# Weights' low part last in each granule, and a new order of products in the gates and the output projection

## The chip, the cores and the metric

The kernel runs on one core of a Trainium2 chip. Its engines are TensorE (PE, which multiplies matrices into the PSUM banks), VectorE (DVE), ScalarE (ACT), GpSimd (POOL) and SyncE (SP); SP and POOL issue the transfers from main memory (HBM). The metric is the device time of one execution in microseconds (us), lower is better.

## The reference

Two layers of a trunk on 512 tokens of 1024 channels, in float32:

```python
def swiglu(x, w_in, w_out):
    gu = x @ w_in
    g, u = jnp.split(gu, 2, axis=-1)
    return (jax.nn.silu(g) * u) @ w_out
...
    f = jnp.fft.fft2(ug, axes=(1, 3), norm="ortho").real
...
    y_na = neighbourhood_attention(q.reshape(shp), k.reshape(shp), v.reshape(shp), rpb) @ w_na_out
    y_f = fourier_mix(uf) @ w_f_out
    g_na = jax.nn.sigmoid(ga + gate_bias[0])
    g_f = jax.nn.sigmoid(gf + gate_bias[1])
    return (g_na * y_na + g_f * y_f) @ w_o
...
    for l in range(DEPTH):
        x = x + 0.5 * swiglu(rms_norm(x, ffn1_norm[l]), ffn1_w_in[l], ffn1_w_out[l])
        x = x + mixer(rms_norm(x, mix_norm[l]), mix_w_in[l], mix_gate_bias[l], na_rpb[l],
                      na_w_out[l], f_w_out[l], mix_w_o[l])
        x = x + 0.5 * swiglu(rms_norm(x, ffn2_norm[l]), ffn2_w_in[l], ffn2_w_out[l])
    return rms_norm(x, final_norm)
```

The hidden width of the feed-forward part (FFN) is 2816. `mix_w_in` makes q, k, v, the Fourier input u and two gates.

## The kernel before

*Two parts for each operand.* Every float32 operand a is split in a high part (a copy on ACT in the type fp32r) and a low part (a minus its high part, on DVE). A product is three matmuls into one sum: high by high, high activation by low weight, low activation by high weight (`mm3`, L333: L334, L335, L336 in this order). In the profile `whi` and `wlo` are the parts of weights, names that end in h and l those of activations.

*Strassen products.* Large products go by 2 x 2 blocks with seven products (1 to 7) for eight. The weights' operands of products 3, 5 and 6 are sums or differences, which are made on the way: on DVE (L182, a `Raw` tile and an `add`), or, where `strassen` (L219) is called with `dma`, by POOL transfers that add into the raw tile in place (`then`, L205; `Raw.plus`, L154).

*The stream of weights.* `stage_items` (L209) lists all granules (128 x 1024 raw numbers, 512 KB) in the order of use. `Stream` (L288) walks that list with four counters: `fetch` issues the loads on SP into a ring of raw tiles (9 in the FFN), `high` does the sum and the copy on ACT, `low` the subtraction on DVE (and the `then` transfer), and `next` hands out a granule after the two behind it have been made (`AHEAD`). `whi` and `wlo` have three buffers each. `negate` (L167) turns the sign of a raw tile on ACT and has POOL add another granule to it; this is done for the odd part of u (`un` minus `um`, tile uo) and for the cosine and sine sums of the Fourier output (`fq`).

*Granules and PE's order.* `product` (L479) takes two k-tiles of 128 in a granule for two PSUM banks, 12 matmuls of 512 columns (6 in a granule of one k-tile). `product_T` (L512) makes a transposed result for the gates, 24 matmuls of 256 columns a granule; with `fine` it is a generator that yields after each granule.

*The stages of a layer.* FFN (in-projection: `plain` in C tiles, then five column blocks in A, B; out-projection W_o, three chunks of k, tile o), mixer, FFN. The order of instructions is a scheduler's in the FFN. In the mixer (from the last part of W_o to the middle of the gates) the orders of DVE, ACT and PE are written by hand: what stands first in the code is first in the queue of its engine. There, in order: `proj_V` (v, whose parts are stored to HBM by SP, L982, and the folded inputs hp, hm, ex), `proj_U` (ue and ux, then uo), q, k and attention in steps `att_step` (L1270: output of head pair i-2, transposes of i-1, scores of i), with the Fourier output (`f_fill`, L1295, tile ef) between the last steps; then the gates: `block` and `block_1` are generators of the products of gate blocks 0 and 1, each `next` one granule or one product's end, with sums for the activations t1, t2, t3 and the rows of n (`fill_n`, tile ps) in between; last the output projection (L1590 to L1620: tiles wA, wB, wC, activations m1 to m7), and `put` adds into x.

The order of the gates' granules before is in one line of `stage_items`, which the sequence of `next(block)` and `next(block_1)` (L1545 to L1582) has to match:

```python
for i, order in ((0, (5,)), (1, (2,)), (0, (6, 7, 3)), (1, (5,)), (0, (4,)), (1, (6, 7, 3, 4))):
```

## Time and profile before

| | us |
|---|---|
| median of 3 runs (lowest to highest) | 1917.12 (1916.45 to 1921.8) |
| the profiled execution's own time | 1919.48 |
| its span in the trace | 1917.7 |
| PE busy, DVE busy, ACT busy | 1879.4, 1507.6, 1166.5 |

The first layer's stages lie so in the span: FFN's in-projection to 225 us, W_o to 338, v and u to 378, attention to 480, gates to 585, output to 610, the second FFN to 960. The second layer follows from 960 in the same order.

How to read it: busy times add up the instructions of an engine; matmuls are pipelined, so that one of 0.39 us is followed by the next after 0.23. A row of waits names the engine, the line and tile that waited, and after the arrow the engine and instruction that ended the wait; then the total, the number and the longest. A row of the timeline has start and duration in us, the engine, the line, the operation, out<-in and, in brackets, the idle time before it.

### The profile page before, as it was taken

The numbers are of one execution on the slowest core, as the hardware profiler recorded it, in microseconds if no ns is written. First come the engines' busy times: TensorE is split into PE (matmuls) and PEld (weight loads), VectorE is DVE, ScalarE is ACT, GpSimd is POOL, SyncE is SP. The second block draws the span as 40 slices with busy tenths as digits, with TensorE's granted clock in tenths as the row PEclk, the third lists the DMA queues.
The fourth block names the chain that finished last, engine by engine and source line by source line (L and its number), as shares of the span: only waits on it lengthen the run. The fifth ranks groups of instructions, "written<-read, shape, count | busy, mean of one in ns | idle before, by whom it ended". The sixth has DMA issues, their size and how long they took to land.

```text
span 1917.7 us, 25845 instructions
## 1 busy us (share of the span) xinstructions
PE 1879.4 (98%) x9609; PEld 1590.5 (83%) x9609; DVE 1507.6 (79%) x1902; ACT 1166.5 (61%) x1726; POOL 176.4 (9%) x212
## 2 busy tenths in 40 slices
PE   9999999999999999999999999999999999999997
PEld 7888888888997888888888888888888978888886
DVE  8767799757868777779977768995677797777898
ACT  6655666757565655566655556666675566555664
POOL 0101011000111000001000100110001110100010
PEclk9999999999999999999999999999999999999998
DMA  8777487855977476759857765977559875776693
GB/s 287 202 200 196 154 245 246 252 155 151 250 198 171 140 194 199 186 150 262 244 142 203 185 182 169 265 245 226 149 168 219 214 192 129 200 184 164 180 284 123
DMA packets 108301, 378.91 MB, mean 198 GB/s; under 512 B 12288, under 2 KB 12416, under 8 KB 108176
## 3 DMA queue, kind: packets, MB, share of 16 engines
q1 hardware_dynamic: 78944, 275.19, 41.2%
q0 software_dynamic: 28800, 101.78, 29.2%
q8 instruction: 75, 1.23, 0.3%
q14 instruction: 50, 0.41, 0.1%
q10 hardware_dynamic: 432, 0.30, 0.0%
HBM read 370.93 MB, written 6.29 MB: 197 GB/s over the span
## 4 chain that ended last, share of the span: by engine, by line
PE 73%; DVE 15%; issue 5%; ACT 4%; DMA 3%; POOL 0%; ACTq 0%; SPq 0%; DVEq 0%; POOLq 0%
PE A L334 7%; PE A L336 7%; PE A L335 7%; DVE wlo L197 5%; PE B L334 4%; PE B L336 4%; PE B L335 4%; PE o L335 3%; DMA raw<-in_wst_dram 3%; PE o L336 3%; PE o L334 3%; PE ps L334 2%; PE ps L336 2%; PE ps L335 2%; PE C L335 2%
## 5 line engine op out<-in xcount | busy, mean ns | idle before, releaser
L197 DVE TENSOR_TENSOR wlo<-raw,whi 128x1024 fp32r<-128x1024 f32 (+2 forms) x524 | 620.0, 1190 | 300.8 <-ACT whi L190 297.4
L190 ACT ACTIVATE whi<-raw 128x1024 fp32r<-128x1024 f32 (+2 forms) x524 | 539.2, 1033 | 441.9 <-PE A L336 116.6
L154 POOL DMA_DIRECT2D raw<-in_wst_dram x162 | 140.4, 875 | 1405.1 <-DMA raw<-in_wst_dram 768.2
L182 DVE TENSOR_TENSOR raw<-raw,raw 128x1024 f32<-128x1024 f32 (+1 forms) x128 | 150.9, 1189 | 2.5
L336 PE MATMUL A<-whi,xl 128*128 128x512 f32 x320 | 124.6, 389 | 0.0
L334 PE MATMUL A<-whi,xh 128*128 128x512 f32 x320 | 124.5, 389 | 0.0
L335 PE MATMUL A<-wlo,xh 128*128 128x512 f32 x320 | 124.5, 389 | 0.0
L188 ACT ACTIVATE whi<-raw 128x1024 fp32r<-128x1024 f32 x76 | 79.1, 1041 | 67.8 <-PE B L336 33.2
L195 DVE SCALAR_TENSOR_TENSOR wlo<-raw,whi 128x1024 fp32r<-128x1024 f32 x76 | 90.5, 1195 | 20.0 <-ACT whi L188 19.8
L543 ACT ACTIVATE sn<-A 128x512 f32<-128x512 f32 x96 | 56.5, 598 | 41.2 <-PE A L336 40.1
L336 PEld LDWEIGHTS A<-whi,xl 128*128 128x128 f32 x320 | 60.1, 188 | 12.5
L335 PEld LDWEIGHTS A<-wlo,xh 128*128 128x128 f32 x320 | 60.1, 188 | 12.5
L334 PEld LDWEIGHTS A<-whi,xh 128*128 128x128 f32 x320 | 60.1, 188 | 12.4
L334 PE MATMUL B<-whi,t1h 128*128 128x512 f32 x160 | 63.7, 398 | 0.0
L335 PE MATMUL C<-wlo,xh 128*128 128x512 f32 x160 | 62.4, 390 | 0.5 <-DVE wlo L197 0.5
L335 PE MATMUL A<-wlo,t2h 128*128 128x512 f32 x160 | 62.4, 390 | 0.4 <-DVE wlo L197 0.4
L334 PE MATMUL A<-whi,t3h 128*128 128x512 f32 x160 | 62.4, 390 | 0.2 <-ACT sn L543 0.2
L334 PE MATMUL C<-whi,xh 128*128 128x512 f32 x160 | 62.2, 390 | 0.2 <-ACT whi L190 0.2
L336 PE MATMUL B<-whi,t1l 128*128 128x512 f32 x160 | 62.4, 390 | 0.0
L335 PE MATMUL A<-wlo,t3h 128*128 128x512 f32 x160 | 62.3, 389 | 0.0
L336 PE MATMUL A<-whi,t2l 128*128 128x512 f32 x160 | 62.3, 389 | 0.0
L335 PE MATMUL B<-wlo,t1h 128*128 128x512 f32 x160 | 62.3, 389 | 0.0
(431 smaller groups left out, 5246.8 us busy)
## 6 DMA issues: line engine op xcount, KB each, us to landing
raw<-in_wst_dram SPq DMA_DIRECT2D x459, 512.0 KB
raw<-in_wst_dram POOLq DMA_DIRECT2D x180, 512.0 KB, 7.8
raw<-in_wst_dram SPq DMA_DIRECT2D x30, 256.0 KB
vc<-vd SPq DMA_DIRECT2D x28, 256.0 KB
bm<-in_near_dram SPq DMA_DIRECT2D x16, 384.0 KB
vd<-v SPq DMA_DIRECT2D x8, 512.0 KB
dft<-in_dft_dram POOLq DMA_DIRECT2D x4, 514.0 KB, 6.6
x<-in_xin_dram SPq DMA_DIRECT2D x4, 512.0 KB
```

The lines of the kernel that those rows point to most:

```text
L154: G.dma_start(out=self.t, in_=wst[GRAN_AT[self.plus]][:, 0 : self.n], accum_op=ALU.add)
L182: V.tensor_tensor(t, t, self.add.t, ALU.add)
L188: S.activation(self.out[0][:, cs], self.raw.t[:, cs], AF.Copy, scale=-1.0)
L190: S.activation(self.out[0][:, cs], self.raw.t[:, cs], AF.Copy)
L195: self.last = V.scalar_tensor_tensor(lo, t, -1.0, hi.bitcast(F32), ALU.mult, ALU.subtract)
L197: self.last = V.tensor_tensor(lo, t, hi.bitcast(F32), ALU.subtract)
L334: PE.matmul(ps, lh, rh, start=start, stop=False, skip_group_check=again)
L335: PE.matmul(ps, lh, rl, start=False, stop=False, skip_group_check=again)
L336: PE.matmul(ps, ll, rh, start=False, stop=stop, skip_group_check=again)
L543: S.activation(t[:, b, :], ps[b], AF.Copy)
```

## The change

`run` takes the place of `mm3` in `product`, `product_T`, `plain`, the last part of W_o, `proj_T`, `proj_V`, `proj_U`, `n_rows` and in half of `f_fill`. It takes a list of terms and first does, for each, high by high and the activation's low part by the weights' high part, and then, for each, the weights' low part:

```diff
+    def run(terms, again=False):
+
+        for ps, lh, ll, rh, rl, w, start, stop in terms:
+            PE.matmul(ps, lh, rh, start=start, stop=False, skip_group_check=again)
+            PE.matmul(ps, *((lh, rl) if w == "l" else (ll, rh)), start=False, stop=False, skip_group_check=again)
+        for ps, lh, ll, rh, rl, w, start, stop in terms:
+            PE.matmul(ps, *((ll, rh) if w == "l" else (lh, rl)), start=False, stop=stop, skip_group_check=again)
```

In `product` the terms of a granule go together, but those of the last granule go bank by bank, so that the first bank ends at its half (`product_T` alike):

```diff
+            if i + n == len(kts):
+                run(terms[0:n], again)
+                run(terms[n:], again)
+            else:
+                run(terms, again)
```

The sum of an item becomes a method of its own, which `low` calls for the next item, if that is loaded, ahead of its own subtraction:

```diff
         def low(self):
+            if self.prepped + 1 == self.highs < self.loaded:
+                self.items[self.highs].sum()
             self.items[self.prepped].low()
```

The gates' products and the output's:

```diff
-            for i, order in ((0, (5,)), (1, (2,)), (0, (6, 7, 3)), (1, (5,)), (0, (4,)), (1, (6, 7, 3, 4))):
+            for i, order in ((0, (5,)), (1, (2,)), (0, (6, 7)), (1, (5,)), (0, (3, 4)), (1, (6, 7, 4, 3))):
...
-            strassen(s, lambda q: "w" + q, 0, two, ORDER, True)
+            strassen(s, lambda q: "w" + q, 0, two, ORDER_W, True)
```

`ORDER_W` is (5, 1, 2, 6, 7, 3, 4), where `ORDER` was (1, 5, 2, 6, 7, 3, 4). For it, the sum of product 3 is not made by a POOL transfer into the tile of product 6 but by a DVE sum with b. In the code of the output, a2 and wB (product 5) now stand ahead of a6 and wA (product 1).

In `proj_V`, at two places of the attention, and in the first FFN, loads, negations and preparations move:

```diff
+            ws.fetch(ws.highs + 5)
             root = norm.roots(0, 2)
...
             h0 = upper(folds[0], "hp")
+            ws.negate()
+            ws.negate()
             done(2, False)
...
             ws.high()
-            ws.negate()
             some((0, 1), VG[2], False, False)
...
             ws.high()
-            ws.negate()
...
         att_step(2)
+        ws.fetch(ws.highs + 5)
+        ws.negate()
         r64, w64 = rows_64()
...
         bias_for(3)
+        ws.fetch(ws.highs + 5)
         ws.negate()
         att_step(4, lambda: ws.prep(ws.pos + 2))
-        ws.negate()
         ws.prep(ws.pos + 3)
...
-        att_step(5, ws.low, mid=lambda: next(f_rows))
-        for _ in range(3):
+        att_step(5, ws.low)
+        for _ in range(4):
             next(f_rows)
         ws.high()
-        att_step(6, ws.low, mid=lambda: next(f_rows))
-        ws.prep(ws.pos + 1)
-        for _ in range(3):
+        next(f_rows)
+        att_step(6, ws.low)
+        for _ in range(5):
             next(f_rows)
         ws.high()
-        att_step(7, ws.low, ws.high, ws.low)
+        att_step(7, ws.low, ws.prep_one)
...
-        fill_n(0, [ws.next(0), ws.next(0)])
+        fill_n(0, [ws.next(0), ws.next(0)], ws.prep_one)
         acts[6] = low(h2, t12, "t2")
-        ws.high()
-        ws.low()
```

`prep_one` is `high` and then `low`; `fill_n` calls it before its third row. `f_fill` yields before it drains a block instead of after it. In the first FFN `ws.prep(ws.pos + 3)` stands one DVE and ACT group earlier. The number of instructions of PE, and of loads on SP, stays.

More of the change, by code (lines that the diff above doesn't have):

```diff
@@ L33 @@
 ORDER_0 = (1, 2, 5, 6, 7, 3, 4)
+ORDER_W = (5, 1, 2, 6, 7, 3, 4)
 FETCH = (8, 4)
@@ L179, in high, with sum @@
                 )
-            t = self.raw.t
-            if self.add:
-                V.tensor_tensor(t, t, self.add.t, ALU.add)
+            self.sum()
             if self.parts == 1:
                 self.upper(slice(0, n))
+        def sum(self):
+            if self.add:
+                V.tensor_tensor(self.raw.t, self.raw.t, self.add.t, ALU.add)
+                self.add = None
         def upper(self, cs):
@@ L217, in strassen @@
         def strassen(s, name, idx, sizes, order, dma=False):
-            r = made.setdefault((s, name("a"), idx), {}) if dma and order[0] > 2 else {}
+            r = made.setdefault((s, name("a"), idx), {}) if dma and len(order) < 7 and order[0] > 2 else {}
             for q, q2 in () if r else (("a", None), ("b", None), ("c", "a"), ("d", "c")):
@@ L231, in strassen @@
                     elif m == 3:
-                        add(d, None if dma else b)
+                        add(d, None if dma and order is not ORDER_W else b)
                     elif m == 4:
@@ L237, in strassen @@
                     elif m == 6:
-                        add(d, None if dma else a, then=b.key if dma else None)
+                        add(d, None if dma else a, then=b.key if dma and order is not ORDER_W else None)
                     else:
@@ L315, in prep, with prep_one @@
                 self.low()
+        def prep_one(self):
+            self.high()
+            self.low()
         def enter(self, stage):
@@ L486, in product @@
             for b in range(2):
+                terms = []
                 for i, kt in enumerate(kts):
@@ L490, in product @@
                     last = stop and i == len(kts) - 1
-                    mm3(ps[b], h[:, kt, c], l[:, kt, c], wh[:, z], wl[:, z], start and i == 0, last, again)
+                    terms.append((ps[b], h[:, kt, c], l[:, kt, c], wh[:, z], wl[:, z], "r", start and i == 0, last))
+                run(terms, again)
                 if hook and b == 0:
@@ L499, in product @@
             wl = wl.rearrange("p (a b) -> p a b", b=T)
+            terms = []
             for b in range(2):
@@ L503, in product @@
                     lh, ll = h[:, kts[i + k], c], l[:, kts[i + k], c]
-                    mm3(
-                        ps[b], lh, ll, wh[:, k, :], wl[:, k, :], start and i + k == 0,
-                        stop and i + k == len(kts) - 1, again,
-                    )
+                    terms.append((
+                        ps[b], lh, ll, wh[:, k, :], wl[:, k, :], "r", start and i + k == 0,
+                        stop and i + k == len(kts) - 1,
+                    ))
+            if i + n == len(kts):
+                run(terms[0:n], again)
+                run(terms[n:], again)
+            else:
+                run(terms, again)
             if hook and i == 0:
@@ L516, in product_T @@
             wh, wl = [z.rearrange("p (a b c) -> p a b c", a=2, c=P) for z in (ws.next(0) if fine else ws.next())]
+            terms = []
             for cb in range(4):
@@ L521, in product_T @@
                     mh, ml = h[:, kt, off : off + 256], l[:, kt, off : off + 256]
-                    first = start and kt == 0
-                    PE.matmul(to, wh[:, k, cb], mh, start=first and cb % 2 == 0, stop=False, skip_group_check=True)
-                    PE.matmul(to, wh[:, k, cb], ml, start=False, stop=False, skip_group_check=True)
-                    PE.matmul(to, wl[:, k, cb], mh, start=False, stop=kt == 3, skip_group_check=True)
+                    first = start and kt == 0 and cb % 2 == 0
+                    terms.append((to, wh[:, k, cb], wl[:, k, cb], mh, ml, "l", first, kt == 3))
+            for n in (slice(0, 4), slice(4, 8)) if g else (slice(0, 8),):
+                run(terms[n], True)
             if fine:
@@ L581, in plain @@
             i, k = divmod(kt, 4)
+            terms = []
             for j in js:
@@ L584, in plain @@
                     t = slice((2 * j + b) * P, (2 * j + b + 1) * P)
-                    mm3(pcl[j][b], hx[i][:, k, t], lx[i][:, k, t], wh[:, c], wl[:, c], kt == 0, kt == DT - 1)
+                    terms.append((pcl[j][b], hx[i][:, k, t], lx[i][:, k, t], wh[:, c], wl[:, c], "r", kt == 0, kt == DT - 1))
+            run(terms)
         for g in range(2):
@@ L613, in stage_ffn @@
                 norm.squares(1, 0)
+            if first:
+                ws.prep(ws.pos + 3)
             V.tensor_tensor(b21, b21, b22, ALU.subtract)
@@ L618, in stage_ffn @@
                 norm.squares(1, 1)
-                ws.prep(ws.pos + 3)
                 norm.rstd()
@@ L755, in granule @@
                 kts = list(range(len(CHUNK[0][c])))[2 * g : 2 * g + 2]
+                terms = []
                 for b in bs:
@@ L758, in granule @@
                         t, z = slice(off + b * P, off + (b + 1) * P), slice(k * T, (k + 1) * T)
-                        mm3(
-                            to[b], h[:, kt, t], l[:, kt, t], w[0][:, z], w[1][:, z], False,
-                            c == 2 and g == 1 and k == len(kts) - 1, True,
-                        )
+                        terms.append((
+                            to[b], h[:, kt, t], l[:, kt, t], w[0][:, z], w[1][:, z], "r", False,
+                            c == 2 and g == 1 and k == len(kts) - 1,
+                        ))
+                run(terms, True)
             m, c, src = steps[i + 2]
@@ L952, in proj_T @@
             wh, wl = ws.next()
+            terms = []
             for kt in range(DT):
                 c = slice(kt * P, (kt + 1) * P)
-                mm3(ps, wh[:, c], wl[:, c], *xs[kt], kt == 0, kt == DT - 1)
+                terms.append((ps, wh[:, c], wl[:, c], *xs[kt], "l", kt == 0, kt == DT - 1))
+            run(terms)
             return ps
@@ L966, in some @@
             def some(cs, g, first, last):
+                terms = []
                 for k, (wh, wl) in enumerate(wide(w[g])):
@@ L970, in some @@
                         lh, ll = [z[:, c * P : (c + 1) * P] for z in xs[kt]]
-                        mm3(pss[c], lh, ll, wh, wl, first and k == 0, last and k == 1)
+                        terms.append((pss[c], lh, ll, wh, wl, "r", first and k == 0, last and k == 1))
+                run(terms)
             vt = {}
@@ L1070, in proj_U @@
                 wh, wl = [z.rearrange("p (a b) -> p a b", b=UC) for z in ws.next(0)]
+                terms = []
                 for n, kt in enumerate(kts):
@@ L1074, in proj_U @@
                         c = slice(b * P, (b + 1) * P)
-                        mm3(
-                            ps[b][:, 0:UC], hp[i][0][:, k, c], hp[i][1][:, k, c], wh[:, n, :], wl[:, n, :],
+                        terms.append((
+                            ps[b][:, 0:UC], hp[i][0][:, k, c], hp[i][1][:, k, c], wh[:, n, :], wl[:, n, :], "r",
                             kt == 0, kt == DT - 1,
-                        )
+                        ))
                     PE.matmul(px[0:2, 0:UC], ex[i][:, k, :], wh[:, n, :], start=kt == 0, stop=False)
+                run(terms)
+                for n, kt in enumerate(kts):
+                    i, k = divmod(kt, 4)
                     PE.matmul(px[0:2, 0:UC], ex[i][:, k, :], wl[:, n, :], start=False, stop=kt == DT - 1)
@@ L1096, in proj_U @@
                 wh, wl = [z.rearrange("p (a b) -> p a b", b=HALF) for z in ws.next(0)]
+                terms = []
                 for b in range(2):
@@ L1099, in proj_U @@
                     for k in range(4):
-                        mm3(
-                            ps[b][:, 0:HALF], hm[g][0][:, k, c], hm[g][1][:, k, c], wh[:, k, :], wl[:, k, :],
+                        terms.append((
+                            ps[b][:, 0:HALF], hm[g][0][:, k, c], hm[g][1][:, k, c], wh[:, k, :], wl[:, k, :], "r",
                             g == 0 and k == 0, g == 1 and k == 3,
-                        )
+                        ))
+                run(terms)
             for b in range(2):
@@ L1190, in bias_for, with att_scores @@
                 bms[hp].append(res)
-        def att_scores(i, after, mid):
+        def att_scores(i, after):
             hp, pr = divmod(i, 2)
@@ L1223, in att_scores @@
                     V.reciprocal(rs[:, 2 * e : 2 * e + 2], sm[:, 2 * e : 2 * e + 2])
-                    if mid and not e:
-                        mid()
             se = s_[0].rearrange("p (a k) -> p a k", a=2)
@@ L1268, in stage_mixer, with att_step @@
         sc, pt_ = {}, {}
-        def att_step(i, then=None, before=None, last=None, mid=None):
+        def att_step(i, then=None, before=None, last=None):
             if 0 <= i - 2 < 8:
@@ L1279, in att_step @@
             if i < 8:
-                sc[i] = att_scores(i, last, mid)
+                sc[i] = att_scores(i, last)
         fs, ns = {}, {}
@@ L1311, in f_fill @@
                         PE.matmul(pe, eh[:, c], pl, start=False, stop=False, skip_group_check=True)
-                        PE.matmul(pe, el[:, c], ph, start=False, stop=False, skip_group_check=True)
                     c = slice(i * T + cb * P, i * T + cb * P + P)
                     PE.matmul(pe, w64[0:68, c], p64[0][0:68, 0:KC], start=False, stop=False, skip_group_check=True)
+                    cs = [slice(gp * T + cb * P, gp * T + cb * P + P) for gp in range(2)]
                     for gp in range(2):
-                        c = slice(gp * T + cb * P, gp * T + cb * P + P)
-                        mm3(po, oh[:, c], ol[:, c], qf[gp][:, 0, :], qf[gp][:, 1, :], False, gp == 1, True)
+                        PE.matmul(pe, el[:, cs[gp]], pf[gp][:, 0, :], start=False, stop=False, skip_group_check=True)
+                    run([(po, oh[:, cs[gp]], ol[:, cs[gp]], qf[gp][:, 0, :], qf[gp][:, 1, :], "l", False, gp == 1) for gp in range(2)], True)
+                    yield
                     t = tmp(s="fo")[:, 0:HALF]
@@ L1323, in f_fill @@
                     V.tensor_tensor(y[:, T - 1 : HALF : -1], pe[:, 1:HALF], t[:, 1:HALF], ALU.add)
-                    yield
+                    if cb == 3:
+                        yield
         def n_rows(w, cb):
             ps = bank()
+            terms = []
             for kt, (h_, l_) in enumerate(o):
@@ L1331, in n_rows, with fill_n @@
                 c = slice(kt % 2 * T + cb * P, kt % 2 * T + cb * P + P)
-                mm3(ps, wh[:, c], wl[:, c], h_, l_, kt == 0, kt == 3)
+                terms.append((ps, wh[:, c], wl[:, c], h_, l_, "l", kt == 0, kt == 3))
+            run(terms)
             return ps
-        def fill_n(i, w):
+        def fill_n(i, w, then):
             for cb in range(4):
+                if cb == 2:
+                    then()
                 if cb % 2 == 0:
@@ L1470, in stage_mixer @@
         ga0, gf0, ga1, gf1 = [None, None], [None, None], [None, None], [None, None]
-        block = gate_block(0, acts, ORDER_0, {6: lambda: fourth()}, ga0, gf0, (1, 2, 5, 6))
-        block_1 = gate_block(1, acts, ORDER_0, {}, ga1, gf1, (1, 2))
+        block = gate_block(0, acts, (1, 2, 5, 6, 7, 3, 4), {6: lambda: fourth()}, ga0, gf0, (1, 2, 5, 6))
+        block_1 = gate_block(1, acts, (1, 2, 5, 6, 7, 4, 3), {}, ga1, gf1, (1, 2))
         ws.high()
-        att_step(5, ws.low, mid=lambda: next(f_rows))
-        for _ in range(3):
+        att_step(5, ws.low)
+        for _ in range(4):
             next(f_rows)
         ws.high()
-        att_step(6, ws.low, mid=lambda: next(f_rows))
-        ws.prep(ws.pos + 1)
-        for _ in range(3):
+        next(f_rows)
+        att_step(6, ws.low)
+        for _ in range(5):
             next(f_rows)
         ws.high()
-        att_step(7, ws.low, ws.high, ws.low)
+        att_step(7, ws.low, ws.prep_one)
         next(block)
@@ L1538, in stage_mixer @@
         ws.high()
+        ws.low()
         V.tensor_tensor(t12, t12, B[1, 1][1], ALU.add)
         next(block_1)
-        ws.low()
         h2 = high(t12, "t2")
-        fill_n(0, [ws.next(0), ws.next(0)])
+        fill_n(0, [ws.next(0), ws.next(0)], ws.prep_one)
         acts[6] = low(h2, t12, "t2")
-        ws.high()
-        ws.low()
         ws.high()
@@ L1577, in stage_mixer @@
         written.pop().__exit__(None, None, None)
-        for _ in range(2):
-            next(block)
+        next(block)
         next(block_1)
+        next(block)
         next(block)
@@ L1589, in stage_mixer @@
         m10, m11 = ga1
-        pa = pair("wA")
-        product(pa, a1, K4, True)
-        put(pa, 0, 0, -1)
-        a6 = combo(m00, m00, m11, ALU.add, "m6")
         a2 = parts(m10, "m2")
@@ L1597, in stage_mixer @@
         put(pb, 1, 1, -1)
+        a6 = combo(m00, m00, m11, ALU.add, "m6")
+        pa = pair("wA")
+        product(pa, a1, K4, True)
+        put(pa, 0, 0, -1)
         V.tensor_tensor(m01, m01, m11, ALU.subtract)
```

## The prediction

> **What bounds the kernel now.** I read first the page's busy times, then the list of what TensorE waited for, then the timeline at the largest of those waits, and last a table of windows by stage.

> ```profile
> span 1917.7 us, 25845 instructions
> PE 1879.4 (98%) x9609; PEld 1590.5 (83%) x9609; DVE 1507.6 (79%) x1902; ACT 1166.5 (61%) x1726; POOL 176.4 (9%) x212
> ```

> TensorE is busy for 98% of the span. The change leaves its 9609 matmuls and 9609 weight loads, so it can win only idle time, and time in which the clock is not full. By the page that is 1917.7 − 1879.4 = 38.3 us idle. Where it lies (columns: total us, times, longest):

> ```profile
> PE o L335 <- DVE wlo L197: 3.7, 7, 0.6
> PE ef L336 <- DVE wlo L197: 3.5, 2, 1.7
> PE B L523 <- ACT whi L190: 3.2, 2, 1.9
> ...
> PE ps L1239 <- DVE s L1227: 2.6, 4, 1.1
> PE uo L335 <- DVE wlo L197: 1.8, 2, 0.9
> PE uo L334 <- ACT whi L190: 1.7, 2, 1.1
> PE B L525 <- DVE wlo L197: 1.5, 2, 0.8
> PE ps L336 <- DVE wlo L197: 0.8, 2, 0.4
> PE wC L334 <- ACT m2h L340: 0.7, 2, 0.3
> PE wB L334 <- ACT whi L190: 0.7, 2, 0.3
> PE ux L1079 <- ACT ex L1048: 0.5, 1, 0.5
> PE C L335 <- DVE wlo L197: 0.5, 1, 0.5
> PE A L335 <- DVE wlo L197: 0.4, 1, 0.4
> ...
> PE C L334 <- ACT whi L190: 0.2, 1, 0.2
> ```

> Most are waits for a weights' low part (wlo), which DVE makes last of all operands of a granule. What one costs shows at the first W_o product with activation c6 (start, duration, instruction, idle before):

> ```profile
> 283.13 0.39 PE L334 MATMUL o<-whi,c6h 128*128 128x512 f32 x1
> ...
> 284.10 0.50 PE L335 MATMUL o<-wlo,c6h 128*128 128x512 f32 x1 [0.59 <-DVE wlo L197]
> ...
> 284.44 0.40 PE L336 MATMUL o<-whi,c6l 128*128 128x512 f32 x1
> 284.67 0.39 PE L334 MATMUL o<-whi,c6h 128*128 128x512 f32 x1
> ```

> Undisturbed matmuls of this shape start 0.23 us apart (284.44 to 284.67). Here one starts 284.10 − 283.13 = 0.97 us after the one before, and the next 0.34 after that. So the wait costs 0.74 + 0.11 = 0.85, the list's 0.59 and 0.26 more. I add 0.26 to every wait listed.

> Beside idle time there are stretches at half clock (columns after the window: us; busy of PE, PEld, DVE, ACT, POOL; granted clock; DMA share; GB/s):

> ```profile
> 460.00:520.00 60.00, 58.22 (x442) 55.48 (x443) 49.23 (x76) 38.78 (x77) 10.44 (x12) 1.00 0.85 225
> 531.00:539.00 8.00, 6.86 (x32) 6.66 (x33) 7.43 (x10) 5.35 (x10) 1.73 (x2) 0.57 0.48 109
> 1323.00:1328.00 5.00, 4.63 (x26) 4.63 (x27) 3.45 (x6) 2.81 (x5) 0.00 (x0) 0.66 1.00 388
> 1484.00:1488.00 4.00, 3.91 (x20) 3.91 (x21) 4.00 (x7) 2.65 (x5) 0.86 (x1) 0.57 0.46 137
> ```

> The first row, with ef's wait of 1.7 us in it, is at full clock. [...]

> **The change part by part.** *Low parts last.* In each granule all products with the high part go first, those with wlo last. In a granule of 12 matmuls the first use of wlo moves from place 2 to place 9, 7 × 0.23 = 1.6 us later; in the last granule of a product, which goes by halves of 6, from 2 to 5, 0.7. The price is that an activation's low part is wanted 0.23 earlier and that wlo's last use is one matmul later, hence its buffer. Matmuls keep their spacing whatever operand stands still: each has its own weight load already, so the new order costs PE nothing by itself.

> W_o has seven waits, 3.7 + 7 × 0.26 = 5.5 us, none over 0.6 listed, 0.85 in full, against 0.7 to 1.6 of new allowance: I take 5.0. The first FFN's three (C, A on wlo, and a 0.2 on whi that its earlier preparation should cover) are 1.1 + 0.8 = 1.9. W_o is also where the sum of the next granule, now done before the current low part, stands at another place in DVE's order; it is the same instruction, so no term of its own. Its cover is thin, since DVE is nearly full there:

> ```profile
> 225.00:338.00 113.00, 111.79 (x509) 92.33 (x508) 109.41 (x126) 73.46 (x94) 13.06 (x16) 1.00 0.80 240
> 560.00:608.00 48.00, 47.28 (x262) 40.49 (x260) 42.12 (x50) 27.38 (x37) 6.38 (x8) 1.00 0.80 192
> L197 DVE TENSOR_TENSOR wlo<-raw,whi 128x1024 fp32r<-128x1024 f32 (+1 forms) x37 | 41.6, 1136 | 2.4 <-ACT whi L190 2.4
> ```

> (The last row is DVE's group of low parts in the first of these windows.)

> *uo, earlier fetch and negation.* The raw weights of uo are loaded by SP behind the store of v, and summed by a POOL transfer after a negation on ACT:

> ```profile
> SPq L982 <- DVE v L981: 21.9, 2, 21.8
> 362.23 0.88 POOL L169 DMA_DIRECT2D raw<-in_wst_dram  x1 [21.31 <-ACT raw L168]
> 370.37 1.06 ACT L190 ACTIVATE whi<-raw 128x1024 fp32r<-128x1024 f32 x1 [1.90 <-DMA raw<-in_wst_dram]
> ```

> The transfer issued at 362.23 landed at 370.37, 8.1 us. Both loads now stand ahead of that store, which held SP for up to 21.8 us, and the negations ahead of at least four ACT instructions of 1.0 us (the copies of two products, h1's high part, a weights' high part), so the sum that landed at 370.4 should land near 366, and ACT waited for it 1.9. What is passed on SP, the v store here and loads of bm at the attention's fetches, comes one 512 KB load later, 2.3 us at the 225 GB/s of the row for 460 to 520; bm is wanted steps later, so I charge nothing, and 2.3 a layer if that cover is gone. All waits on uo and the one on ux go: 1.8 + 1.7 + 0.5 + 5 × 0.26 = 5.3, and the half-clock stretch at 1323 with them, 1.4. Together 6.7; I take 6.4.

> *Gates' third product.* Its two waits in each layer are B on whi and on wlo, 3.2 + 1.5 + 4 × 0.26 = 5.7, with stretches at 531 and 1484 worth 2.8 + 1.4 = 4.2:

> ```profile
> 529.04 0.28 PE L524 MATMUL B<-xl,whi 128*128 128x256 f32 x1
> 529.16 0.28 PE L525 MATMUL B<-xh,wlo 128*128 128x256 f32 x1
> 531.38 0.39 PE L523 MATMUL B<-xh,whi 128*128 128x256 f32 x1 [1.94 <-ACT whi L190]
> ...
> 532.64 0.58 PE L525 MATMUL B<-xh,wlo 128*128 128x256 f32 x1 [0.76 <-DVE wlo L197]
> ACT whi L190 <- DMA raw<-in_wst_dram: 5.4, 1, 5.4
> raw<-in_wst_dram POOLq DMA_DIRECT2D x4, 512.0 KB, 9.3
> ```

> The high part waited 5.4 us for one of four POOL transfers (last row, median 9.3 to land). Behind block 1's fifth product, 48 matmuls that start 0.12 apart (529.04 to 529.16), the third is wanted 5.8 us later, more than 1.94 + 0.76. The transfers of block 1's own sums, and one for the output product's first, now queue on POOL before others of block 1, 9.3 us each in turn, but block 1's third product, which needs the last, is now the last of all; its seventh runs straight into the fourth on one accumulator, and must wait for the subtraction on DVE (0 hidden, up to 1.22, the longest DVE row below); for that I charge 0.6 a layer. Term: 5.7 + 4.2 − 1.2 = 8.7.

> *Attention's filling.* ef and s are 3.5 + 2.6 + 6 × 0.26 = 7.7 over two layers. The weights' chain was:

> ```profile
> 459.02 1.08 ACT L340 ACTIVATE p<-ps 128x512 fp32r<-128x512 f32 x2
> 459.92 1.22 DVE L197 TENSOR_TENSOR wlo<-raw,whi 128x1024 fp32r<-128x1024 f32 x1
> ```

> The negations leave the ACT work ahead of it, about one instruction of 1.0 each, but the low part still stands behind the attention output on DVE. Bounds: nothing, or 3.8 a layer; I take 1.4 a layer, 2.8, near the lower since ef's wait is the larger and stays mostly.

> *Rows of n.* DVE had, up to the wait on the last:

> ```profile
> 491.14 1.22 DVE L1500 TENSOR_TENSOR t1l<-t,t1h 128x1024 fp32r<-128x1024 f32 x1
> 492.36 1.23 DVE L197 TENSOR_TENSOR wlo<-raw,whi 128x1024 fp32r<-128x1024 f32 x1
> ```

> The new order puts one such instruction of 1.22 more before two of the low parts, while low-last gives 0.5 to 1.4. Bounds: 0.8 a layer won (0.4 + 0.26, and what hangs on it), or 1.7 lost; I take 0.9 lost, 1.8 in all.

> *Output product.* wC and wB, 0.7 + 0.7 + 4 × 0.26 = 2.4, should go, as m2's parts are now made ahead of two products and m6's sum ahead of one, and a product is 24 matmuls of 0.23, 5.5 us. Four POOL sums become DVE adds, two a layer. At 1.22 (the first row of the last fence) they are 4.9 us on DVE, which has 48 − 42.1 = 5.9 idle in the stretch of a layer: hidden, 0; unhidden 4.9. I take them as hidden, and the term as 2.4. The raw tiles of these adds also hold their buffers longer, so some later load starts later; that is in the allowance below.

> Sum: 5.0 + 1.9 + 6.4 + 8.7 + 2.8 − 1.8 + 2.4 = 25.4. Against it stand waits that a list of today's can't name, above all on DVE's new order: none, or, by the dearest that I charge above (0.9 a layer in n) at two more places in each layer, 3.6; I take 2.4, nearer that end. Net 23 us. The profiled execution took 1919.5 (span 1917.7 and 1.8 around it), 2.4 over the median of 1917.1. It would take 1896.5; from the median, the forecast is **1894**.

> The half-clock rows stand each right after waits of 1.94 + 0.76, 0.5 + 1.1 + 0.9 and 1.3 + 0.8. [...]

> **The rivals.**
> (1) *Half clock stays*, for instance set off by other waits (ef, 1.7, at a place where n or the gates add to it). For: two of the three stretches came after waits of at most 1.3 each, and ef's is 1.7. Against: ef's own set off none. Time 1894 + 5.6 = 1900.
> (2) *DVE becomes the bound* in W_o and the output product. For: 109.4 of 113 us. Then W_o's 5.0 and the output's 2.4 are not won and the four adds cost 4.9: 1894 + 12.3 = 1906. Against: in the W_o window DVE's own idle is behind ACT's whi, not PE.
> (3) *The transfers slide along*: uo and the third product wait for data (POOL, 9.3 us, in turn), and earlier issue only lengthens their queue. Then 6.4 + 8.7 are lost: 1909. Against: at 524 to 531 only four transfers were under way.
> (4) *Slower: low parts block DVE.* Three wlo buffers; each is now free one matmul (0.23) later, and everything behind a waiting low part on DVE waits too. The W_o window has 37 low parts and there are four such stages: 148 × 0.23 = 34 us, time 1928. It turns the sign once the mean is over 23 / 148 = 0.16 us. Against: today DVE is the late one there, 2.4 us idle in 37, so it hardly finds a buffer still in use.

> **How the numbers follow.** Chances: forecast 0.63, (1) 0.08, (2) 0.13, (3) 0.09, (4) 0.07. A difference of 0.3%, 5.8 us, is about what can be told from none, so *same* is 1911.4 to 1922.9. Faster: 0.63 + 0.08 + 0.11 of (2) + 0.05 of (3) = 0.87; same the rest of these, 0.06, and a little of (4): 0.07; slower 0.06. The low end takes no new waits and n at its better bound: 23 + 2.4 + 3.4 of n + 3 of ef = 32, 1885. The high end reaches over (2) to (3), 1910.

> **What would show it.** In the changed kernel's list of waits: o on wlo (3.7) under 0.8; uo and ux gone; B on whi and wlo gone, and the granted clock at full through 520 to 560; ef still some 1.8 a layer; ps of the n rows larger, about 1 a layer; wC and wB gone. PE's instructions stay at 9609. Wrong would be: a new wait of PE on wlo in W_o (2), B or uo still waiting behind a transfer (3), DVE idle before wlo with PE as releaser (4), half clock away from these places (1).

## The result and the profile after

| | before | changed |
|---|---|---|
| median, us (4 runs each) | 1917.02 | 1905.56 |
| lowest to highest, us | 1916.45 to 1921.8 | 1903.99 to 1907.35 |
| profiled execution, us (its span) | 1919.48 (1917.7) | 1903.99 (1902.2) |

The ratio is 0.9935 (95% interval 0.9916 to 0.9954): faster, by 11.5 us between the medians where 23 was forecast, and inside the stated range. The two profiled executions lie 15.5 apart; before's was above its median and the changed kernel's was its fastest.

From the page of the changed kernel:

```profile
span 1902.2 us, 25942 instructions
PE 1874.4 (99%) x9609; PEld 1587.8 (83%) x9609; DVE 1513.3 (80%) x1906; ACT 1163.3 (61%) x1726; POOL 172.9 (9%) x208
```

PE's instructions are the same; DVE has four more and POOL four fewer. The changed kernel's list of what PE waited for (total us, times, longest; lines have moved, L351, L352 and L354 are high by high, low activation and low weight):

```profile
PE wB L351 <- ACT whi L194: 3.7, 2, 1.9
...
PE ef L354 <- DVE wlo L201: 2.9, 2, 1.5
PE ps L354 <- DVE wlo L201: 1.4, 2, 0.9
PE C L354 <- DVE wlo L201: 1.2, 2, 0.6
PE ps L1280 <- DVE s L1268: 0.9, 4, 0.3
PE A L351 <- ACT sn L570: 0.6, 2, 0.4
PE o L354 <- DVE wlo L201: 0.4, 1, 0.4
PE ps L351 <- ACT whi L194: 0.2, 1, 0.2
```

Without the warm-up's 3.2, the list went from 22.5 to 11.3 us. Gone are uo, ux, B, wC and all but one wait of o. At the top is now wB, 1.9 in each layer, which had 0.7 in both before and which the prediction had gone. The windows of the changed kernel where half clock was or is (columns as in the prediction, the granted clock third from the end):

```profile
520.00:560.00 40.00, 39.56 (x324) 38.85 (x323) 29.71 (x33) 23.99 (x37) 6.18 (x7) 1.00 0.87 229
602.00:605.00 3.00, 3.00 (x8) 2.34 (x7) 3.00 (x4) 1.06 (x1) 0.00 (x0) 0.50 0.87 294
1323.00:1328.00 5.00, 5.00 (x34) 3.89 (x34) 2.35 (x8) 2.09 (x5) 0.00 (x0) 1.00 0.52 182
1484.00:1488.00 4.00, 4.00 (x36) 4.00 (x35) 1.97 (x3) 2.50 (x4) 0.87 (x2) 1.00 0.37 142
```

The three old stretches are at full clock; one new one stands behind the wait of wB in the first layer.

To lay the terms of the prediction beside the trace, I took from both traces how much later each matmul starts than its shape's undisturbed spacing (0.227 us for 512 columns, 0.120 for 256, 0.109 for transposes), counted what is over 0.095, kept matmuls in half clock apart, and added by stage, over both layers:

| stage | lost before + half clock | lost after + half clock | gained | forecast |
|---|---|---|---|---|
| first FFN, in-projection | 2.6 | 1.2 | 1.4 | 1.9 |
| W_o, four stages | 5.5 | 1.1 | 4.4 | 5.0 |
| v, ue, ux, uo | 5.2 + 1.4 | 0 | 6.6 | 6.4 |
| attention and Fourier filling | 12.6 | 10.9 | 1.7 | 2.8 |
| gates and rows of n | 9.4 + 4.2 | 9.3 | 4.3 | 8.7 − 1.8 |
| output projection | 3.1 | 4.3 + 1.6 | −2.8 | 2.4 |

The gains add up to 15.6, against 15.5 between the spans.

### The profile page after: what moved, and what is told of

Read it like the earlier page. It is cut to its first block, busy times and chain, and to the rows that moved or that the text cites. A ratio compares the mean times of both kernels' runs of the same rounds, so it can differ in the third digit from the quotient of the medians.

```text
span 1902.2 us, 25942 instructions
## 1 busy us (share of the span) xinstructions
PE 1874.4 (99%) x9609; PEld 1587.8 (83%) x9609; DVE 1513.3 (80%) x1906; ACT 1163.3 (61%) x1726; POOL 172.9 (9%) x208
## 3 DMA queue, kind: packets, MB, share of 16 engines
q8 instruction: 75, 1.23, 0.3%
## 4 chain that ended last, share of the span: by engine, by line
PE 85%; DVE 6%; ACT 5%; DMA 2%; issue 2%; SPq 0%; ACTq 0%; DVEq 0%
PE A L351 9%; PE A L352 8%; PE A L354 8%; PE o L351 7%; PE o L352 7%; PE o L354 7%; PE B L354 4%; PE B L351 4%; PE B L352 4%; PE ps L354 2%; PE ps L351 2%; PE ps L352 2%; PE tr L593 2%; DMA raw<-in_wst_dram 2%; PE C L354 2%; PE C L351 2%
## 5 line engine op out<-in xcount | busy, mean ns | idle before, releaser
L187 DVE TENSOR_TENSOR raw<-raw,raw 128x1024 f32<-128x1024 f32 (+1 forms) x132 | 156.8, 1192 | 2.4
L351 PE MATMUL A<-whi,xh 128*128 128x512 f32 x320 | 124.5, 389 | 0.0
L352 PE MATMUL A<-whi,xl 128*128 128x512 f32 x320 | 124.5, 389 | 0.0
L677 ACT ACTIVATE th<-sn,r 128x512 f32<-128x512 f32 x80 | 57.1, 716 | 75.4 <-DVE sn L575 75.4
L354 PE MATMUL A<-wlo,xh 128*128 128x512 f32 x320 | 92.1, 389 | 0.0
L354 PEld LDWEIGHTS A<-wlo,xh 128*128 128x128 f32 x320 | 60.1, 188 | 12.5
L352 PEld LDWEIGHTS A<-whi,xl 128*128 128x128 f32 x320 | 60.1, 188 | 12.5
L351 PEld LDWEIGHTS A<-whi,xh 128*128 128x128 f32 x320 | 60.1, 188 | 12.5
L351 PE MATMUL B<-whi,t1h 128*128 128x512 f32 x160 | 63.8, 399 | 0.0
L351 PE MATMUL A<-whi,t2h 128*128 128x512 f32 x160 | 62.5, 391 | 0.0
L352 PE MATMUL B<-whi,t1l 128*128 128x512 f32 x160 | 62.4, 390 | 0.0
L351 PE MATMUL A<-whi,t3h 128*128 128x512 f32 x160 | 62.4, 390 | 0.0
L352 PE MATMUL A<-whi,t2l 128*128 128x512 f32 x160 | 62.3, 389 | 0.0
L352 PE MATMUL A<-whi,t3l 128*128 128x512 f32 x160 | 62.3, 389 | 0.0
L351 PE MATMUL B<-whi,xh 128*128 128x512 f32 x160 | 62.3, 389 | 0.0
L351 PE MATMUL C<-whi,xh 128*128 128x512 f32 x160 | 62.2, 389 | 0.0
## 6 DMA issues: line engine op xcount, KB each, us to landing
raw<-in_wst_dram SPq DMA_DIRECT2D x459, 512.0 KB
raw<-in_wst_dram POOLq DMA_DIRECT2D x176, 512.0 KB, 8.1
vd<-v SPq DMA_DIRECT2D x8, 512.0 KB
x<-in_xin_dram SPq DMA_DIRECT2D x4, 512.0 KB
```

The lines of the kernel that those rows point to most:

```text
L187: V.tensor_tensor(self.raw.t, self.raw.t, self.add.t, ALU.add)
L351: PE.matmul(ps, lh, rh, start=start, stop=False, skip_group_check=again)
L352: PE.matmul(ps, *((lh, rl) if w == "l" else (ll, rh)), start=False, stop=False, skip_group_check=again)
L354: PE.matmul(ps, *((ll, rh) if w == "l" else (lh, rl)), start=False, stop=stop, skip_group_check=again)
L677: S.activation(th[:, b, :], g[:, b, :], AF.Silu, scale=norm.r[:, c : c + 1])
```

## The experiments

Each kernel was timed in five rounds beside the kernel before on the same chip. Before's median was 1918.35 us beside e1, e2, e4 and e5, 1917.39 beside the changed kernel's second timing, e6, e12 and e13, and 1919.18 beside the rest; so the ratios, not the medians, are compared.

**The changed kernel again.**

> The changed kernel unaltered, beside the others of this set. Theory (its gain is some 13 us and single executions scatter by a few us, since a wait at the end of W_o and half clock come and go): a ratio to before of 0.992 to 0.995. Rival (the profiled pair's 15.5 us is the gain): 0.991 to 0.992.

1904.96 us, ratio 0.9932 (0.9916 to 0.9948): the gain is 12.4 us between the medians and 13 by the ratio, and the profiled pair's 15.5 was a little lucky. In this execution half clock followed wB's wait in both layers (mean granted clock 0.996, against 0.997 in the first).

**Low parts last alone (e1).** `run` in place of `mm3`, and nothing else:

```diff
-                    mm3(
-                        ps[b], lh, ll, wh[:, k, :], wl[:, k, :], start and i + k == 0,
-                        stop and i + k == len(kts) - 1, again,
-                    )
...
+                run(terms, again)
```

> The kernel before with one part of the change: weights' low parts last in each granule, everything else as before. Theory (the order alone covers late low parts): the seven waits of o on wlo in W_o and those of the first FFN go (5.8 us by the two traces), uo's and B's waits on wlo go too (about 4), their waits on whi stay; 1907 to 1909. Rival (the new order holds wlo's buffers longer and DVE gives the time back): within 2 us of before, 1915 to 1919.

1915.16 us, ratio 0.9986 (0.9976 to 0.9996): hardly more than the rival's. Its list of waits:

```profile
PE A L341 <- ACT sn L560: 6.7, 4, 3.3
PE ps L1270 <- DVE s L1258: 3.7, 4, 1.4
...
PE wA L341 <- ACT whi L190: 2.1, 2, 1.1
PE o L344 <- DVE wlo L197: 2.1, 1, 2.1
PE C L341 <- ACT whi L190: 1.7, 1, 1.7
```

B's waits on wlo went, and of W_o's seven (3.7 in all) one is left, but that one is 2.1 long. Others came for what stands next: A in the gates waits up to 3.3 for the copy (sn) out of its PSUM bank, and C and wA wait for whi. The order alone moves the waits to the next late operand.

**All but low parts last (e2).**

```diff
         for ps, lh, ll, rh, rl, w, start, stop in terms:
-            PE.matmul(ps, lh, rh, start=start, stop=False, skip_group_check=again)
-            PE.matmul(ps, *((lh, rl) if w == "l" else (ll, rh)), start=False, stop=False, skip_group_check=again)
-        for ps, lh, ll, rh, rl, w, start, stop in terms:
-            PE.matmul(ps, *((ll, rh) if w == "l" else (lh, rl)), start=False, stop=stop, skip_group_check=again)
+            mm3(ps, lh, ll, rh, rl, start, stop, again)
...
```

The Fourier filling (`f_fill`) goes back to its old order of matmuls too.

> The changed kernel with the three matmuls of a term in a row again, all else of the change kept. Theory: the waits on wlo come back, 5.8 us in W_o and the first FFN and about 4 in gates and n rows; 1913 to 1917. Rival (early loads, the gates' order and the sums one granule ahead did it): 1905 to 1908.

1913.5 us, ratio 0.9971 (0.9961 to 0.9981): as the theory had it. Waits on wlo are back:

```profile
PE C L346 <- DVE wlo L201: 3.6, 4, 1.5
...
PE o L345 <- DVE wlo L201: 2.7, 5, 0.8
PE A L346 <- DVE wlo L199: 2.1, 4, 0.8
```

So the low order is worth 0.0014 alone and 0.0037 (0.9971 less 0.9934, the mean of the changed kernel's two) beside the rest, 3 and 7 us.

**The output projection undone (e4).** Order 1, 5, 2, 6, 7, 3, 4 and product 3's sum by POOL again.

> The changed kernel with the output projection as before (order 1, 5, 2, 6, 7, 3, 4, product 3's sum by a POOL transfer). Theory (the new wait of wB on whi, 1.9 us a layer behind DVE's sum, and the half clock after it, are a loss of the output's new order): the trace's 2.15 a layer go and at most 0.7 a layer of the old waits come back; 1901 to 1904. Rival (DVE is late there whatever the order, since low-last moved it): within 1.5 us of the changed kernel, 1904 to 1907.

1903.89 us, ratio 0.9927 (0.9913 to 0.9942), beside 0.9935 and 0.9932 of the changed kernel: inside the theory's span of times, but no difference that the intervals tell apart. wB's wait is gone and wA waits for its high part instead; counted as in the table, the stage loses 3.1 us, what it lost before:

```profile
PE o L354 <- DVE wlo L201: 2.2, 1, 2.2
PE wA L351 <- ACT whi L194: 2.0, 2, 1.0
```

**The gates undone (e5).**

```diff
-            for i, order in ((0, (5,)), (1, (2,)), (0, (6, 7)), (1, (5,)), (0, (3, 4)), (1, (6, 7, 4, 3))):
+            for i, order in ((0, (5,)), (1, (2,)), (0, (6, 7, 3)), (1, (5,)), (0, (4,)), (1, (6, 7, 3, 4))):
```

> The changed kernel with the gates' products in the old order (block 0: 6, 7, 3 before block 1's 5; block 1 ending 3, 4). Theory (the move of the third product is what removed B's waits and the half clock after them): B waits on whi 1.3 to 1.9 a layer again and half clock follows in one layer at least; 1908 to 1912. Rival (low-last alone covers it): 1904 to 1907.

1912.45 us, ratio 0.9973 (0.9963 to 0.9984), some 7.5 us over the changed kernel: about the theory's time. But its trace, taken of the slowest of its twelve executions (1918.57 us), has no half clock in the gates, and PE hardly waits at B:

```profile
PE A L351 <- ACT sn L570: 5.7, 4, 2.5
...
PE B L351 <- ACT whi L194: 0.2, 1, 0.2
```

In ACT's queue the copy of A out of PSUM stands behind the high part that waits for a POOL transfer; the timeline of ACT in this kernel:

```profile
552.24 1.06 ACT L194 ACTIVATE whi<-raw 128x1024 fp32r<-128x1024 f32 x1 [2.86 <-DMA raw<-in_wst_dram]
553.20 0.58 ACT L570 ACTIVATE sn<-A 128x512 f32<-128x512 f32 x1
```

The cause is the late transfer in both kernels; the place where PE feels it is what follows on ACT.

**The uo part undone (e6).** No fetch ahead of v's store, negations in their old places.

> The changed kernel without the fetch ahead of v's store and with the negations of uo back in their old places. Theory (that is what removed the waits on uo and ux, 5 us by the traces, and half clock after them in one layer): 4 to 7 us above the changed kernel, waits of uo on whi in both layers; wlo's wait stays covered by the low parts being last. Rival (low-last covers it): at most 2 us above.

1907.69 us, ratio 0.994 (0.9924 to 0.9956), 1 to 3 us over the changed kernel and not apart from it by the intervals. Its trace lost 2.4 us in W_o, ahead of the edited place, and half clock followed there. No wait of uo is listed, though ACT still waits 3.1 us there for the transfers; what is left is one on ux:

```profile
PE ux L1116 <- ACT ex L1084: 0.5, 1, 0.5
```

e1 has none on uo either, so the early loads aren't needed for most of this term once the low parts come last. But e2, which has the early loads and the old order of the three matmuls, has no wait of uo or ux either: one of the two parts is enough. Without the early loads the cover is thin: in e6 uo's first high part is ready 0.32 and 0.23 us before PE starts on it in the two layers. Why it comes earlier there than in the kernel before (31.1 us after v's first matmul in the first layer, against 31.9) I did not settle.

**The update of x first (e12).** The stage where the changed kernel loses most, its output projection; first DVE, then PE:

```profile
597.70 1.22 DVE L201 TENSOR_TENSOR wlo<-raw,whi 128x1024 fp32r<-128x1024 f32 x1
598.83 1.23 DVE L187 TENSOR_TENSOR raw<-raw,raw 128x1024 f32<-128x1024 f32 x1
599.97 1.23 DVE L201 TENSOR_TENSOR wlo<-raw,whi 128x1024 fp32r<-128x1024 f32 x1
601.11 1.29 DVE L1671 SCALAR_TENSOR_TENSOR x<-wA,x 128x512 f32<-128x512 f32 x2
```

```profile
597.92 0.62 PE L354 MATMUL wA<-wlo,m6h 128*128 128x512 f32 x2
...
601.29 0.58 PE L351 MATMUL wB<-whi,m3h 128*128 128x512 f32 x1 [1.87 <-ACT whi L194]
...
602.94 0.63 PE L351 MATMUL wA<-whi,m7h 128*128 128x512 f32 x1
```

Product 6 ends about 598.5. Product 7 adds onto the same bank, so the update of x (601.11 to 602.4) must have read it first, and the scheduler has put that behind two low parts and the sum. It also put four matmuls of product 3 ahead of product 7 on PE, and these wait for that sum. One edit:

```diff
-        put(pa, 0, 1, -1)
+        with tc.high_priority():
+            put(pa, 0, 1, -1)
```

> The changed kernel with one edit: in the output projection the update of x after product 6 goes before the next granules' low parts and sum on DVE (a higher priority for the scheduler). PE's seventh product adds onto the same bank and so waits for that update, which came at 601.1 to 602.4, behind two low parts and the new sum, while product 6 ended at 598.6. Theory (the sum on DVE delays the update, and that is the output's 2.15 us a layer): the wait of wB goes, 3 to 6 us below the changed kernel. Rival (DVE is full there, so the wait moves to the low parts of product 7): within 1.5 us of it.

1897.97 us, ratio 0.9901 (0.9883 to 0.9919), 6 to 7 us below the changed kernel. In e12 the update runs as soon as a bank is done, and product 7 starts at once:

```profile
595.99 0.69 DVE L1672 SCALAR_TENSOR_TENSOR x<-wA,x 128x512 f32<-128x512 f32 x1
...
597.35 0.69 DVE L1672 SCALAR_TENSOR_TENSOR x<-wA,x 128x512 f32<-128x512 f32 x1
597.96 1.22 DVE L201 TENSOR_TENSOR wlo<-raw,whi 128x1024 fp32r<-128x1024 f32 x1
599.09 1.22 DVE L187 TENSOR_TENSOR raw<-raw,raw 128x1024 f32<-128x1024 f32 x1
```

```profile
597.15 0.39 PE L351 MATMUL wA<-whi,m7h 128*128 128x512 f32 x1
```

No wait of the output is left in e12's list and no half clock in its trace, except at the very end: the granted clock is 1.00 in its windows of the output, 570 to 608 and 1513 to 1550, where the changed kernel has 0.96 and 1.00.

**POOL's sum with the update first (e15).** As e12, with `then=b` back and no DVE sum for product 3.

> e12 (the update of x after product 6 first) with the sum for product 3 made again by a POOL transfer, so DVE has four adds less. Theory (once the update goes first, the adds are hidden): within 1.5 us of e12. Rival (DVE is the bound of the output stage, so the adds cost their 4.6 us): 3 to 5 us below e12. If the transfer lands too late, wB waits on whi behind a transfer instead.

1900.41 us, ratio 0.9901 (0.9884 to 0.9917), that of e12: once the update goes first, the adds show no cost, though either interval reaches some 3 us to each side.

**Three low parts earlier (e13), and one more (e16).** e13 is e12 and, in each place, `ws.low()` moved ahead of what stood before it:

```diff
+        ws.low()
         next(f_rows)
-        att_step(6, ws.low)
+        att_step(6)
...
-        att_step(8, ws.low)
+        ws.low()
+        att_step(8)
...
-        V.tensor_tensor(t12, t12, B[1, 1][0], ALU.add)
         next(block_1)
         ws.high()
         ws.low()
+        V.tensor_tensor(t12, t12, B[1, 1][0], ALU.add)
```

> As e12, and three low parts earlier on DVE: fq's ahead of the drain of a Fourier block (ef waits 1.45 a layer), that of block 0's product 6 ahead of the attention's output (C waits 0.6 a layer), and that of the n rows ahead of the first sum of t2 (ps waits 0.4 to 0.9). Theory (these waits are DVE's order alone): ef, C and ps on wlo all but go, 5 to 7 us below e12. Rival (what is put behind them on DVE is late instead): new waits of the same size, within 2 us of e12.

1896.24 us, ratio 0.9883 (0.9865 to 0.9901). ef, C and ps on wlo are gone from its list, 6.0 us of e12's, and A came in their place. The gain over e12 is 3.5 us by the ratios (0.0018) and 1.7 between the medians, and the intervals overlap: less than the theory's 5 to 7, and not told apart from the rival.

> e13 and one more step of the same kind: the low part of the gates' first granule ahead of the last Fourier block's drain, the next granule ahead of the attention's transposes, for A's waits of 0.7 and 0.3 on wlo that e13 has in each layer. Theory (DVE's order again): A's waits on wlo under 0.5 in all, 1 to 2 us below e13. Rival (the transposes' work is late instead): no gain.

1895.32 us, ratio 0.988 (0.986 to 0.99): no gain over e13 that shows, the rival. First e13's line, then e16's:

```profile
PE A L354 <- DVE wlo L199: 2.0, 5, 0.7
```

```profile
PE ps L1280 <- DVE s L1268: 3.0, 6, 1.0
```

**No sum one granule ahead (e7).** `low` without its first two lines.

> The changed kernel without the sum one granule ahead: each sum is again made when its granule's high part is. Theory (in W_o DVE is full, so where its sums stand moves waits but wins little): within 2 us of the changed kernel. Rival (the sum ahead is what shortened W_o): at least 3 us above, with several waits of o on whi or wlo.

1909.45 us, ratio 0.9953 (0.9936 to 0.997), 0.002 or 4 us over the changed kernel, though the intervals overlap: the rival's size, but not its place. o waits 2.8, as it does in kernels with the hoist (2.2 in e4); new are A on whi in the first FFN and, again, product 7 behind the update:

```profile
PE wA L349 <- DVE x L1669: 2.8, 2, 1.4
PE o L352 <- DVE wlo L201: 2.8, 3, 2.3
...
PE A L349 <- ACT whi L194: 1.2, 2, 0.6
```

Here no sum stands ahead of that update, only two low parts (DVE, then PE):

```profile
602.02 2.35 DVE L201 TENSOR_TENSOR wlo<-raw,whi 128x1024 fp32r<-128x1024 f32 x2
604.29 1.28 DVE L1669 SCALAR_TENSOR_TENSOR x<-wA,x 128x512 f32<-128x512 f32 x2
```

```profile
605.12 0.47 PE L349 MATMUL wA<-whi,m7h 128*128 128x512 f32 x1 [1.39 <-DVE x L1669]
```

**W_o without sums (e14).** In W_o the weights of products 3, 5 and 6 are taken as loaded wherever a sum on DVE makes them (products 3 and 6); product 5 needs none. The kernel then computes something else.

> The changed kernel, where the weights of W_o's products 3, 5 and 6 are taken without their sums, so DVE does 12 adds of 1.13 us less in each of four W_o stages and the output is another. Theory (W_o is bound by DVE in its last part, which is why o still waits for wlo at activation c4, 0.4 to 2.3 us): the wait at c4 goes in every stage, 1 to 3 us below the changed kernel, and FFN's cl after it starts no later. Rival (c4 waits for a transfer): the wait stays, within 1 us.

1901.48 us, ratio 0.9908 (0.9891 to 0.9926), some 5 us below the changed kernel, more than the theory's 1 to 3. No wait of o is in its list. The windows of W_o, the changed kernel's first:

```profile
225.00:334.00 109.00, 108.53 (x490) 89.38 (x489) 105.82 (x120) 67.97 (x87) 14.31 (x19) 1.00 0.84 250
850.00:960.00 110.00, 110.00 (x503) 91.53 (x502) 107.32 (x121) 71.02 (x97) 12.84 (x15) 1.00 0.85 248
```

```profile
225.00:334.00 109.00, 109.00 (x496) 90.45 (x495) 95.81 (x109) 69.14 (x88) 14.59 (x19) 1.00 0.74 199
```

DVE (the third pair of numbers) falls from 105.8 to 95.8 of 109 us and the wait at c4 is gone. The sums' loads fell away or came later too (250 to 199 GB/s), so a share of the transfers in this is not excluded.

## Why the prediction was right in direction and twice too large

*What bounds the kernel, and that low order is free on PE:* right. PE has 9609 matmuls and 9609 weight loads in both; in both, the start after a matmul of 512 columns comes 0.227 us later (median) for each of the three lines of a term. What was won is idle time and clock.

*W_o, 5.0:* 4.4 in the profiled pair, but not a fixed number. The instructions up to the end of the first W_o are those of e4 to e6 too, and there PE lost, from start to start, 1.96 to 2.42 us at c4 in their one trace each, where the changed kernel lost 0.57, and its second timing, e12, e13, e15 and e16 0.34 to 0.90. What decides between the two groups stays open. DVE is full in that stage (105.8 of 109 us), so late parts collect at its last activation. In e14, which frees DVE and some of the transfers, the wait is gone. Here the second rival was partly right.

*uo, 6.4:* the size was right (6.6), the reason only half: the early loads and negations do remove the waits (e2), but without them nearly all of the gain stays (e6), since the new order of the three matmuls removes them as well.

*First FFN, 1.9, and attention, 2.8:* 1.4 and 1.7. Ef's wait fell by 0.6 in all, the rest is s; that ef would mostly stay was said.

*Gates, 8.7, less 1.8 for n:* 4.3. The rows of n did get worse, from 0.8 to 1.6 listed (ps on wlo and whi), less than the 1.8 that was priced. B's waits and half clock went as forecast, and e5 puts the order's worth at some 7.5 us; in e1, with the old order, A waited 3.42 and 3.01 us from start to start in block 0's seventh product, just ahead of the third, with half clock behind both. What failed is the price of the new neighbours, 0.6 a layer at one place. There, where block 1's seventh product runs into the fourth, PE lost 0.1; the losses came elsewhere. C waits for a low part behind attention output and a sum on DVE, block 1's seventh product for sn, the copy of A, ps for its low parts; together the stages lose 9.3 us, as before, and only the half clock's 4.2 is won. The row for C in the changed kernel:

```profile
478.86 0.63 PE L354 MATMUL C<-xh,wlo 128*128 128x256 f32 x3 [0.62 <-DVE wlo L201]
```

e13 shows that the waits of C and ps for low parts are DVE's order: moved ahead, these are in time.

*Output projection, 2.4:* the step that failed, −2.8 in the profiled pair. The prediction took the adds as hidden by 5.9 us of idle DVE time in the stretch, and e15 agrees for the adds alone. It did not ask what stands behind them in DVE's queue: the update of x, for which the next product on that PSUM bank waits. The adds are only a part of this: with the two low parts alone ahead of the update (e7) PE still lost 1.56 us a layer at product 7, where it lost 2.04 at wB with a sum between them. e12 brings the stage to no loss at all, and the kernel to 1898, within 4 us of the forecast.

*New waits, 2.4, and half clock:* half clock followed four of ten waits of 2.03 or 2.04 us (below), which the sum had not priced. For the old stretches the 5.6 was right (1.4 + 4.2 in the table), but as the author's estimate: the granted clock of the three windows gives 8 × 0.43 + 5 × 0.34 + 4 × 0.43 = 6.9, and no run shows a reason to take 5.6 of it. What before's trace shows is 60 matmuls of 256 columns in these stretches, which started 0.213 us apart, against 0.120 at full clock: 60 × 0.093 = 5.6.

*The rivals.* (1) half clock away from the old places did come, behind wB; (2) held in the two stages it named, by a smaller amount. That its time, 1906, is the one measured is luck: W_o's term was mostly won in the profiled pair, and a part of what is missing lies in the gates. (3) hardly: uo came in time, and though ACT still waited 5.2 us for transfers in block 1 of the first layer, the copy queued behind them cost PE only 0.56; (4) did not: in W_o DVE waits for ACT (2.8 us in 225 to 334, all for whi), not for PE.

## What to carry to other kernels

When work is added to a nearly full engine, look not only for idle time to hide it, but for what is queued behind it there and who waits for that: a read of PSUM that frees a bank goes first (6 to 7 us in e12). Giving each late operand more time moves the waits on to the next late one; count a removed wait as won only when the engine that was late has slack in that stage. Between kernels whose waits differ by 2 us at single places, compare medians of several executions: one pair of traces here overstated the gain by a fifth to a third.

## What the runs showed of the hardware

A wait cost twice in some places. In the fourteen traces, apart from their start and end, half clock (0.50 granted) came in stretches of 3.413 us (once two in a row, the 6.83 us from 531.95 in the kernel before), each beginning within 1.8 us of the end of a wait and costing 1.4 to 1.7 us. Waits are counted here from start to start, less the shape's spacing. Among single waits over 1 us, none between 1.0 and 1.75 was followed by one, unless a second wait of 0.9 to 1.2 us came right after it; one of 1.84 us, ef's in e2, was, with small delays beside it. Of the ten waits of 2.03 or 2.04 us at wB four were, the other six not, in programs that are alike there. These two rows are the same wait in the changed kernel, 1.87 listed in each layer, followed by half clock in the first layer (the row for 602 to 605 above, 0.50) and by none in the second:

```profile
1544.00:1547.00 3.00, 3.00 (x14) 2.42 (x14) 3.00 (x4) 0.91 (x1) 0.00 (x0) 1.00 0.91 318
```
